# Scaling both banks of a projection into SBUF at once in a hybrid decoder block, with earlier key copies and a longer pause in an inversion

## The chip, the cores and the metric

The kernel runs on one core of one Trainium2 chip. The metric is the device time of one execution in microseconds (us); a kernel's time is the median of several executions.

## What is computed

One decoder layer on 256 tokens with 16 meta tokens put in front (T = 272), width 2048, 16 heads of 128 in each branch, all in float32. The part of the reference that the change touches is the gated DeltaNet branch: the projections of queries, keys and values go through a causal convolution over four tokens and SiLU, and then through a chunked recurrence.

```python
p = rms_norm(h, mix_norm_g) @ w_in
qkv = jax.nn.silu(causal_depthwise_conv(qkv, conv_w))
q, k = l2_normalize(q), l2_normalize(k)
a_mat = jnp.where(strict, jnp.einsum('bhncd,bhnsd->bhncs', k_beta, k) * decay, 0.0)
sol = triangular_solve(a_mat + eye, concat([v * beta, k_beta * exp(g)]))   # unit lower
def step(S, inp):
    v_new = w_val_c - jnp.einsum('bhck,bhkv->bhcv', w_key_c, S)
    o = q_dec_c @ S + qk_c @ v_new
    return S * g_last_c + k_dec_c.T @ v_new, o
```

Beside it stand a forgetting-attention branch (the names with fox), two output projections merged by sigmoid gates, and an MLP with squared ReLU.

## The kernel before

**Matmuls in two parts.** Every weight tile `raw` (128 x 1024) is split into a rounded part `wh` (ScalarE copy, L82) and a rest `wl` (VectorE subtraction, L131); the pool holds three of each, so a `wh` can be written only when TensorE has read the one three tiles earlier for the last time. The activations `u` are split likewise. `gemm_ws` streams 256 weight columns, two heads, over 16 k-tiles into a pair of PSUM banks `acc`, with three matmuls for a k-tile and bank (L168, L169, L170). There are four such banks, two pairs: a gemm writes the banks of the gemm before the last one, and can start in a bank only when that bank has been read.

**Order of the gemms.** Eight for keys, mixed with eight for the fox queries, then eight for queries, eight for V, eight for the fox keys and so on to the MLP.

**Small work between.** What follows a gemm is written as Python generators in a list `tasks`. After each k-tile `pump()` takes one step of each; `pause(n)` lets n steps go by, `until(...)` waits for other tasks. A scheduler then fixes one order of instructions for each engine. Within an engine the order is fixed; between engines semaphores hold it together.

**From bank to convolution.** `conv_silu` multiplies the bank by the row norms `RU` into an SBUF tile `ca` (VectorE, L465), which is the bank's last reader, copies `ca` scaled into `cv` (ScalarE, L82), adds three shifted terms (VectorE, L470) and applies Silu (ScalarE, L472). `ca`, `cv` and the V result `vt` come from a pool of 12 tiles called t272; `kb`, `S`, `y` and other 128-wide tiles from a pool of 10 called t128; a new tile waits until the readers of the one whose buffer it takes are done.

**The V stage.** `value_head` runs once for each head. The odd head of a pair first goes through `pause(10)`, so that its bank is read late. Then come the convolution, a DMA `vb<-vt` and a DMA `kb<-kT` on GpSimd's queue (L90; they copy bits into tiles that TensorE may transpose), transposes by matmul (`flip`, L94) of vb and vs, later of ks and kb, the copies `vnm` and `V` out of PSUM (VectorE, L757, L758), and the recurrence: S, rhs, y, the output in QT and its squares `jk` (ScalarE, L814).

**The inversion.** `invert` solves the 32 x 32 diagonal blocks on VectorE, writes them to DRAM (dY) and back on SyncE's queue (L536, L539), pauses 18 steps, and then builds the larger blocks with small matmuls (L552).

Of the kernel before, what the change touches and what calls it, by code (L numbers as in the profile page):

```python
# [33 lines left out]
def hybrid_block(ctx: ExitStack, tc: tile.TileContext, x, meta_tokens, mix_norm_g, w_in, conv_w, a_log,  # L34
# [23 lines left out]
    def tt(shape, name, dtype=F32):  # L58
        n = 1
        for d in shape[1:]:  # L60
            n *= d
        for size, tag in ((128, "t128"), (272, "t272"), (512, "t512")):
            if n <= size:
                return tmp.tile(shape, dtype, name=name, tag=tag, bufs=TMP_BUFS[tag])
        raise ValueError(n)
# [15 lines left out]
    def acopy(out, in_, scale=1.0):  # L81
        act.activation(out=out, in_=in_, func=AF.Copy, scale=scale)  # L82
# [5 lines left out]
    def bits(src, shape, name, queue=None):  # L88
        dst = tt(shape, name, F32R)
        (queue or nc.gpsimd).dma_start(out=f(dst), in_=src)  # L90
        return dst
# [5 lines left out]
    def stack(dst, src, both):  # L97
        n = list(src.shape)
        one = 1 if both == (0, 2) else 2
        acopy(dst[..., both[0]:both[1] + 1:both[1] - both[0], :], src.unsqueeze(len(n) - 1).broadcast_to(n[:-1] + [2, n[-1]]))  # L100
        dve.tensor_tensor(out=dst[..., one, :], in0=src, in1=f(dst[..., 0, :]), op=ALU.subtract)
# [16 lines left out]
    def until(*names):  # L118
        while not all(n in done for n in names):
            yield  # L120

    def pause(n):
        for _ in range(n):
            yield
# [332 lines left out]
    tasks.append(small_columns())  # L457


    def conv_silu(dst, acc, ct, n, lead):  # L460
        w = [cwT[:, k, ct:ct + 1] for k in range(4)]
        ca, cv = tt([P, T], "ca"), tt([P, T], "cv")
        m = n - lead
        with tc.high_priority():
            dve.tensor_tensor(out=ca[:, 0:n], in0=acc[:, 0:n], in1=RU[:, T - n:T], op=ALU.mult)  # L465
        acopy(cv[:, 0:m], ca[:, lead:n], scale=w[3])
        for d in range(1, 4):
            yield
            off = max(0, d - lead)
            dve.scalar_tensor_tensor(out=cv[:, off:m], in0=ca[:, lead + off - d:n - d], scalar=w[3 - d],  # L470
                                     in1=cv[:, off:m], op0=ALU.mult, op1=ALU.add)
        act.activation(out=dst, in_=cv[:, 0:m], func=AF.Silu)  # L472
# [45 lines left out]
    def invert():  # L518
        I = big_tile([P, 4352], "I")
        N3 = I[:, 0:1024].rearrange("p (r c) -> p r c", c=32)  # L520
        Y3 = I[:, 1024:2048].rearrange("p (r c) -> p r c", c=32)
        YT = I[:, 2048:4096].rearrange("p (a c) -> p a c", c=64)
        dA = dram.tile([4, HT, 32, 32], F32, name="dA")
        for b in range(4):
            nc.sync.dma_start(out=dA[b].rearrange("a r c -> r a c"), in_=XT3[q[b], :, q[b]])
        nc.sync.dma_start(out=N3, in_=dA.rearrange("b a r c -> (b a) r c"))
        identity(Y3, 32)
        yield from pause(18)
        yield from substitute(N3, Y3, I[:, 4096:4352], 32, P)
        dve.tensor_copy(out=N3, in_=Y3.rearrange("p a b -> p b a"))  # L530
        dY = dram.tile([2, 4, HT, 32, 32], F32, name="dY")
        nc.sync.dma_start(out=dY[0].rearrange("b a r c -> (b a) r c"), in_=Y3)
        nc.sync.dma_start(out=dY[1].rearrange("b a r c -> (b a) r c"), in_=N3)
        pool.memset(YT[0:32, :, 32:64], 0.0)
        for b in range(4):
            nc.sync.dma_start(out=XT3[q[b], :, q[b]], in_=dY[0, b].rearrange("a r c -> r a c"))  # L536
            if b < 3:
                cs = slice(32, 64) if b == 1 else slice(0, 32)
                nc.sync.dma_start(out=YT[q[b], :, cs], in_=dY[1, b].rearrange("a r c -> r a c"))  # L539
        yield from pause(18)  # L540

        B1 = [I[:, i * 256:(i + 1) * 256].rearrange("p (a c) -> p a c", c=32) for i in range(2)]
        B2 = [I[:, 1024 + i * 512:1536 + i * 512].rearrange("p (a c) -> p a c", c=64) for i in range(2)]
        G4 = HT // 8
        for step in range(G4 + 3):
            g = [step - i if 0 <= step - i < G4 else None for i in range(4)]
            p1 = ps_tile()[:, 0:256].rearrange("p (a c) -> p a c", c=32)
            p2 = ps_tile()[:, 0:256].rearrange("p (a c) -> p a c", c=32)
            p3 = ps_tile().rearrange("p (a c) -> p a c", c=64)

            def mm(o_, a_, b_):
                pe.matmul(o_, a_, b_, start=True, stop=True)  # L552

            def idx(x, i):
                return 8 * g[x] + i


            for i in range(8):
                if g[2] is not None:
                    mm(p3[hi, i, :], XT3[lo, idx(2, i), hi], YT[lo, idx(2, i), :])  # L560
                if g[3] is not None:
                    mm(p3[lo, i, :], B2[g[3] % 2][hi, i, :], XT3[hi, idx(3, i), hi])
            for i in range(8):
                if g[0] is not None:
                    for b in (0, 2):
                        mm(p1[q[b + 1], i, :], XT3[q[b], idx(0, i), q[b + 1]], YT[q[b], idx(0, i), 0:32])
                if g[1] is not None:
                    b1 = B1[g[1] % 2]
                    mm(p2[q[0], i, :], b1[q[1], i, :], XT3[q[1], idx(1, i), q[1]])
                    mm(p2[q[2], i, :], b1[q[3], i, :], XT3[q[3], idx(1, i), q[3]])  # L570
                    mm(p2[q[1], i, :], XT3[q[1], idx(1, i), q[1]], b1[q[1], i, :])
            js = [slice(8 * x, 8 * x + 8) if x is not None else None for x in g]
            if g[0] is not None:
                for b in (1, 3):
                    acopy(B1[g[0] % 2][q[b]], p1[q[b]])
            if g[1] is not None:
                acopy(XT3[q[0], js[1], q[1]], p2[q[0]], scale=-1.0)
                acopy(YT[q[1], js[1], 0:32], p2[q[1]], scale=-1.0)
                acopy(XT3[q[2], js[1], q[3]], p2[q[2]], scale=-1.0)
            if g[2] is not None:  # L580
                acopy(B2[g[2] % 2][hi], p3[hi])
            if g[3] is not None:
                acopy(XT3[lo, js[3], hi], p3[lo], scale=-1.0)
            yield from pause(3)
        done.add("XT")
# [24 lines left out]
        done.add("XTm")  # L610

    def key_pair(hp, accs):
        for c in range(2):
            h = 2 * hp + c
            yield from conv_silu(kT[:, h, :], accs[c], 16 + h, T, 0)
            if c == 0:
                yield from pause(2)
        yield from pause(4)
# [76 lines left out]
    def query_pair(hp, accs):  # L695
        dst = [QT[:, 2 * hp + c, :] for c in range(2)]
        if "XT" not in done:

            dst = [tt([P, 256], "qt") for c in range(2)]
        for c in range(2):  # L700
            yield from conv_silu(dst[c], accs[c], 2 * hp + c, 260, 4)
            if c == 0:
                yield from pause(2)
        yield from pause(4)
        if "XT" not in done:
            yield from until("XT")
            for c in range(2):
                acopy(QT[:, 2 * hp + c, :], dst[c])
        qb = bits(QT[:, 2 * hp:2 * hp + 2, :], [P, 2, 256], "qb")
        yield from pause(5)  # L710
        ps = ps_tile()
        for c in range(2):
            for t in range(2):
                flip(ps[:, (2 * c + t) * P:(2 * c + t + 1) * P], qb[:, c, t * P:(t + 1) * P])
        for c in range(2):
            for t in range(2):
                jk = tt([P, P], "jk")
                act.activation(out=jk, in_=ps[:, (2 * c + t) * P:(2 * c + t + 1) * P], func=AF.Square,
                               accum_out=ssq[:, t, 2 * hp + c:2 * hp + c + 1])
# [16 lines left out]

    def value_head(h, acc):
        pace = 4
        yield from pause(10 * (h % 2))
        vt = tt([P, T], "vt")  # L740
        yield from conv_silu(vt, acc, 32 + h, T, 0)
        vb = bits(vt[:, NM:T], [P, 256], "vb")
        vs, ks = [tt([P, 3, NM], name, F32R) for name in ("vs", "ks")]
        stack(vs, vt[:, 0:NM], (0, 2))
        stack(ks, kT[:, h, 0:NM], (0, 2))
        kk = [kT[:, h, NM + t * P:NM + (t + 1) * P] for t in range(2)]
        qq = [QT[:, h, t * P:(t + 1) * P] for t in range(2)]
        yield from pause(3)
        yield from until("k", "XT", "XTm")
        kb = bits(kT[:, h, NM:NM + P], [P, P], "kb")  # L750
        ps = ps_tile()
        for t in range(2):
            flip(ps[:, t * P:(t + 1) * P], vb[:, t * P:(t + 1) * P])
# [425 lines left out]
```

## Time and profile before

| | |
|---|---|
| time, median of 3 executions | 1991.64 us (1990.89 to 1992.62) |
| the profiled execution's own time | 1992.09 us |
| its span, first to last instruction | 1990.3 us |
| mean granted TensorE clock | 0.997 |
| TensorE busy | 1966.9 us, 99% |
| VectorE, ScalarE, GpSimd busy | 60%, 51%, 6% |

The time of an execution is its span and under 2 us around it. TensorE's clock has two levels; a granted clock of 1.00 in a stretch is the upper one throughout, 0.50 the lower one.

### The profile page before, as it was taken

To read this page: it belongs to the slowest core of one execution; us is meant where nothing else is said; L and a number is where in the kernel's file an instruction comes from. 1 tells how busy PE (TensorE), PEld (TensorE's weight loads), DVE (VectorE), ACT (ScalarE), POOL (GpSimd) and SP (SyncE) were. 2 spreads that over 40 slices of the span, in tenths; PEclk is the share of its full clock that TensorE was granted. 3 is DMA by queue.
4 is the path that set the end of the run, shared out by engine and by line. 5 is a ranking of instruction groups with operands and counts; after the bars stand their busy time and mean duration, and the time that the engine had idled before them with its cause. 6 is when DMAs were issued, how large, how long until landed. Compare 5 with 4: busy or idle time off the path is not lost.

```text
span 1990.3 us, 30185 instructions
## 1 busy us (share of the span) xinstructions
PE 1966.9 (99%) x11974; PEld 1735.0 (87%) x11974; DVE 1200.4 (60%) x2005; ACT 1008.2 (51%) x1797; POOL 115.1 (6%) x168
## 2 busy tenths in 40 slices
PE   8999999999999999999999999999999999999998
PEld 7898999999999998888888888888888888888886
DVE  5786846677546776644444555566655456665555
ACT  5644466556555555444444445555543345554444
POOL 0022100011131110000000000000000000000000
PEclk9999999999999999999999999999999999999999
DMA  6556766544566545656565666666655566666555
GB/s 201 171 162 204 217 179 205 165 140 141 182 210 198 165 165 200 203 190 201 190 201 190 201 243 212 199 188 188 188 191 193 197 194 186 188 186 212 196 197 176
DMA packets 283139, 378.77 MB, mean 190 GB/s; under 512 B 24163, under 2 KB 190406, under 8 KB 282470
## 3 DMA queue, kind: packets, MB, share of 16 engines
q1 hardware_dynamic: 275584, 353.65, 56.3%
q0 software_dynamic: 7200, 22.92, 3.5%
q8 instruction: 94, 1.54, 0.3%
q14 instruction: 47, 0.39, 0.1%
q10 hardware_dynamic: 214, 0.28, 0.0%
HBM read 351.63 MB, written 3.76 MB: 179 GB/s over the span
## 4 chain that ended last, share of the span: by engine, by line
PE 93%; issue 3%; DMA 2%; DVE 1%; ACT 0%; SPq 0%; POOL 0%; POOLq 0%; DVEq 0%; ACTq 0%
PE acc L165 15%; PE acc L183 15%; PE acc L185 15%; PE acc L184 15%; PE acc L170 14%; PE acc L168 7%; PE acc L169 7%; PE ps L94 1%; DVE wl L131 1%; DMA kb<-kT 1%; PE ps L552 0%; DMA rawS<-in_w_in_dram 0%; PE ps L896 0%; PE ps L628 0%; DMA dY<-I 0%
## 5 line engine op out<-in xcount | busy, mean ns | idle before, releaser
L131 DVE TENSOR_TENSOR wl<-raw,wh 128x1024 fp32r<-128x1024 f32 x644 | 787.7, 1224 | 635.1 <-ACT wh L82 631.8
L82 ACT ACTIVATE wh<-raw 128x1024 fp32r<-128x1024 f32 x644 | 682.1, 1060 | 751.8 <-PE acc L185 463.7
L170 PE MATMUL acc<-u,wl 128*128 128x272 f32 (+2 forms) x1536 | 440.5, 290 | 0.6 <-DVE wl L131 0.6
L168 PE MATMUL acc<-u,wh 128*128 128x272 f32 (+1 forms) x1280 | 373.0, 293 | 1.0 <-DVE ca L465 1.0
L169 PE MATMUL acc<-u,wh 128*128 128x272 f32 (+1 forms) x1280 | 371.8, 291 | 0.0
L165 PE MATMUL acc<-v,wh 128*128 128x512 f32 x1024 | 355.8, 396 | 0.0
L170 PEld LDWEIGHTS acc<-u,wl 128*128 128x128 f32 x1536 | 289.6, 189 | 3.2 <-DVE wl L131 1.2
L170 PE MATMUL acc<-v,wl 128*128 128x256 f32 x1024 | 279.3, 279 | 0.0
L168 PEld LDWEIGHTS acc<-u,wh 128*128 128x128 f32 x1280 | 241.6, 189 | 2.3 <-DVE ca L465 1.5
L169 PEld LDWEIGHTS acc<-u,wh 128*128 128x128 f32 x1280 | 243.0, 190 | 0.7 <-issue 0.2
L165 PEld LDWEIGHTS acc<-v,wh 128*128 128x128 f32 x1024 | 189.5, 188 | 42.8
L184 PE MATMUL acc<-wl,h1h 128*128 128x512 f32 x504 | 196.1, 389 | 0.0
L185 PE MATMUL acc<-wh,h1l 128*128 128x512 f32 x504 | 196.1, 389 | 0.0
L170 PEld LDWEIGHTS acc<-v,wl 128*128 128x128 f32 x1024 | 192.9, 188 | 3.5
L183 PE MATMUL acc<-wh,h1h 128*128 128x512 f32 x504 | 176.3, 389 | 0.0
L185 PE MATMUL acc<-wh,u 128*128 128x512 f32 x384 | 151.6, 395 | 0.0
L184 PE MATMUL acc<-wl,u 128*128 128x512 f32 x384 | 151.1, 394 | 0.0
L183 PE MATMUL acc<-wh,u 128*128 128x512 f32 x384 | 139.2, 396 | 0.0
L183 PEld LDWEIGHTS acc<-wh,h1h 128*128 128x128 f32 x504 | 94.6, 188 | 19.8
L185 PEld LDWEIGHTS acc<-wh,h1l 128*128 128x128 f32 x504 | 94.6, 188 | 19.6
L184 PEld LDWEIGHTS acc<-wl,h1h 128*128 128x128 f32 x504 | 94.6, 188 | 19.4
L165 PE MATMUL acc<-u,wh 128*128 128x512 f32 x256 | 89.5, 395 | 0.0
(378 smaller groups left out, 2387.8 us busy)
## 6 DMA issues: line engine op xcount, KB each, us to landing
raw<-in_w_in_dram SPq DMA_DIRECT2D x142, 1024.0 KB, 5.2
raw<-in_w_down_dram SPq DMA_DIRECT2D x66, 1024.0 KB, 5.2
raw<-in_w_up_dram SPq DMA_DIRECT2D x64, 1024.0 KB, 5.8
raw<-in_w_o_gdn_dram SPq DMA_DIRECT2D x16, 1024.0 KB, 5.2
raw<-in_w_o_fox_dram SPq DMA_DIRECT2D x16, 1024.0 KB, 5.4
raw<-in_w_out_dram SPq DMA_DIRECT2D x16, 1024.0 KB, 5.3
vb<-vt POOLq DMA_DIRECT2D x32, 128.0 KB, 2.2
tb<-tl POOLq DMA_DIRECT2D x16, 208.0 KB, 2.2
```

Of the source, the lines that this page charges most:

```text
L82: act.activation(out=out, in_=in_, func=AF.Copy, scale=scale)
L94: pe.transpose(out=out.bitcast(F32R), in_=in_, identity=identr)
L131: dve.tensor_tensor(out=wl, in0=raw, in1=f(wh), op=ALU.subtract)
L165: pe.matmul(accs[c][:, 0:2 * n].rearrange("p (a n) -> p a n", a=2), wh[:, s], m[kt // 8][:, kt % 8, :, n0:n1], start=(kt == 0), stop=False)
L168: pe.matmul(o, wh[:, s], part(m, kt, 0, n0, n1), start=(kt == 0), stop=False)
L169: pe.matmul(o, wh[:, s], part(m, kt, 1, n0, n1), start=False, stop=False)
L170: pe.matmul(o, wl[:, s], part(m, kt, 0, n0, n1), start=False, stop=(kt == KT - 1))
L183: pe.matmul(accs[t], a, wh, start=(kt == 0), stop=False)
L184: pe.matmul(accs[t], a, wl, start=False, stop=False)
L185: pe.matmul(accs[t], b, wh, start=False, stop=(kt == nkt - 1 - (last if t else 0)))
```

## The change

`normalized` takes the multiplication by `RU` out of `conv_silu`. The three callers run it for both banks of the pair before the first convolution; for a V head it now stands ahead of the odd head's `pause(10)`. The two `ca` tiles of a pair are thus asked for together. In `value_head` the DMA that fills `kb` stands ahead of `pause(3)` and of the wait for the inversion. The second pause in `invert` is 20 steps. The number of instructions of each kind stays the same.

```diff
+    def normalized(acc, n):
+
+        ca = tt([P, T], "ca")
         with tc.high_priority():
             dve.tensor_tensor(out=ca[:, 0:n], in0=acc[:, 0:n], in1=RU[:, T - n:T], op=ALU.mult)
+        return ca
+
+    def conv_silu(dst, ca, ct, n, lead):
+        w = [cwT[:, k, ct:ct + 1] for k in range(4)]
+        cv = tt([P, T], "cv")
+        m = n - lead
         acopy(cv[:, 0:m], ca[:, lead:n], scale=w[3])
...
-        yield from pause(18)
+        yield from pause(20)
...
     def key_pair(hp, accs):
+        cas = [normalized(acc, T) for acc in accs]
         for c in range(2):
             h = 2 * hp + c
-            yield from conv_silu(kT[:, h, :], accs[c], 16 + h, T, 0)
+            yield from conv_silu(kT[:, h, :], cas[c], 16 + h, T, 0)
...
+        cas = [normalized(acc, 260) for acc in accs]
         for c in range(2):
-            yield from conv_silu(dst[c], accs[c], 2 * hp + c, 260, 4)
+            yield from conv_silu(dst[c], cas[c], 2 * hp + c, 260, 4)
...
     def value_head(h, acc):
         pace = 4
+        ca = normalized(acc, T)
         yield from pause(10 * (h % 2))
         vt = tt([P, T], "vt")
-        yield from conv_silu(vt, acc, 32 + h, T, 0)
+        yield from conv_silu(vt, ca, 32 + h, T, 0)
...
+        yield from until("k")
+        kb = bits(kT[:, h, NM:NM + P], [P, P], "kb")
...
         yield from until("k", "XT", "XTm")
-        kb = bits(kT[:, h, NM:NM + P], [P, P], "kb")
```

The line numbers of the changed kernel differ: the multiplication into `ca` is L464 there, the V copies L766 and L767, the recurrence L780 to L823.

**TensorE between two V gemms.** In the kernel before, one gemm (acc_5616 and acc_5617, the last weight tile wh_5827) passes into the next (acc_5894) like this:

```order
L168 MATMUL acc_5616<-u1_141,wh_5827 128x272
L169 MATMUL acc_5616<-u1_141,wh_5827 128x272
L170 MATMUL acc_5616<-u1_141,wl_5828 128x272
L168 MATMUL acc_5617<-u1_141,wh_5827 128x272
L785 MATMUL ps_5673<-ptm0_4209 128x128
L169 MATMUL acc_5617<-u1_141,wh_5827 128x272
L170 MATMUL acc_5617<-u1_141,wl_5828 128x272
L806 MATMUL ps_5704<-y_5632,kq_5228 128x128
L799 MATMUL ps_5709<-rhs_5637,XT_171 128x128
L168 MATMUL acc_5894<-u0_140,wh_5898 128x272
```

Behind the last L170 of acc_5617 two small matmuls stand. In the changed kernel the same gemm's banks are called acc_5618 and acc_5619, and the next gemm's acc_5896. Its last L170 is followed by the eight rows L800, L801, L794, L814, L815, L780, L786 x2 and L808 of the recurrence, and then by:

```order
L800 MATMUL ps_5636<-S_5567,kT_170 128x128
L801 MATMUL ps_5636<-S_5567,QT_3030 128x128
L94 MATMUL ps_5642<-identr_94,vb_5578 128x128 x2
L94 MATMUL ps_5642<-identr_94,vs_5580 48x128
L800 MATMUL ps_5669<-S_5597,kT_170 128x128
L801 MATMUL ps_5669<-S_5597,QT_3030 128x128
L794 MATMUL ps_5675<-ptm0_4209 128x128
L815 MATMUL ps_5708<-y_5634,kq_5230 128x128
L808 MATMUL ps_5713<-rhs_5639,XT_171 128x128
L94 MATMUL ps_5717<-identr_94,ks_5581 48x128
L94 MATMUL ps_5717<-identr_94,kb_5586 128x128
L168 MATMUL acc_5896<-u0_140,wh_5900 128x272
```

From the last matmul of one gemm to the first of the next there are 20 small rows now; the transposes of vb_5578 and vs_5580, which before stood among the gemm's last k-tiles, are between the gemms.

**ScalarE at the same place.** Before, around the Silu of the odd head (vt_5537), whose DMA fills vb_5578:

```order
L814 ACTIVATE jk_5524,oss_3032<-QT_3030 128x128
L82 ACTIVATE y_5528<-ps_5526 128x128
L82 ACTIVATE kd_5535<-ps_5530,kds_164 128x128
L82 ACTIVATE wh_5827<-raw_5757 128x1024
L472 ACTIVATE vt_5537<-cv_5539 128x272
L82 ACTIVATE S_5567<-ps_5565 128x128
L82 ACTIVATE vs_5580<-vt_5537 128x2x16
L82 ACTIVATE ks_5581<-kT_170 128x2x16
L82 ACTIVATE wh_5898<-raw_5896 128x1024
```

And in the changed kernel (vt_5539; wh_6039 takes the buffer of wh_5827, which the gemm's last matmuls read):

```order
L823 ACTIVATE jk_5526,oss_3032<-QT_3030 128x128
L82 ACTIVATE y_5530<-ps_5528 128x128
L82 ACTIVATE kd_5537<-ps_5532,kds_164 128x128
L82 ACTIVATE wh_6039<-raw_6037 128x1024
L82 ACTIVATE S_5567<-ps_5565 128x128
L477 ACTIVATE vt_5539<-cv_5540 128x272
L82 ACTIVATE QT_3030<-ps_5559,eG_165 128x128
L82 ACTIVATE ptm0_4209<-ps_5602,kds_164 48x128
L82 ACTIVATE xs0_4211<-XTs_173 48x48
L82 ACTIVATE vs_5580<-vt_5539 128x2x16
L82 ACTIVATE ks_5581<-kT_170 128x2x16
```

The Silu stood behind wh_5827 and now stands behind wh_6039, a weight tile of the next gemm.

**VectorE ahead of a gemm's start.** Before, the multiplication that frees the second bank for acc_5617 (ca_5538, from acc_5061) stood behind the V copies of the even head:

```order
L101 TENSOR_TENSOR ks_5411<-kT_170,ks_5411 128x16
L794 SCALAR_TENSOR_TENSOR rhs_5461<-ps_5458,neG_166,V_5192 128x128
L757 CAST vnm0_4207<-ps_5466 48x128
L758 TENSOR_TENSOR V_5470<-ps_5466,nrk_177 128x256
L809 SCALAR_TENSOR_TENSOR S_5494<-S_5289,eGl_163,ps_5491 128x128
L812 TENSOR_TENSOR QT_3030<-ps_5491,QT_3030 128x128
L773 SCALAR_TENSOR_TENSOR ptm1_4210<-ps_5499,kds_164,ptm1_4210 16x128
L780 SCALAR_TENSOR_TENSOR kq_5506<-ps_5503,cst_176,DT_168 128x128
L465 TENSOR_TENSOR ca_5538<-acc_5061,RU_139 128x272
```

Now the one that frees the first bank for acc_5896 (ca_5649, from acc_5340) stands behind the V copies of the odd head:

```order
L782 SCALAR_TENSOR_TENSOR ptm0_4209<-ps_5602,kds_164,ptm0_4209 16x128
L101 TENSOR_TENSOR vs_5580<-vt_5539,vs_5580 128x16
L101 TENSOR_TENSOR ks_5581<-kT_170,ks_5581 128x16
L803 SCALAR_TENSOR_TENSOR rhs_5639<-ps_5636,neG_166,V_5368 128x128
L766 CAST vnm1_4208<-ps_5642 48x128
L767 TENSOR_TENSOR V_5646<-ps_5642,nrk_177 128x256
L464 TENSOR_TENSOR ca_5649<-acc_5340,RU_139 128x272
L803 SCALAR_TENSOR_TENSOR rhs_5672<-ps_5669,neG_166,V_5194 128x128
L821 TENSOR_TENSOR QT_3030<-ps_5708,QT_3030 128x128
L464 TENSOR_TENSOR ca_5654<-acc_5341,RU_139 128x272
```

What moved: before, only the second bank of a gemm was freed behind such V copies; now both banks of a gemm are.

## Rows read from the trace of the kernel before

**Rows 1.** The page, part 1: busy us (share of the span) and count, TensorE.
```profile
PE 1966.9 (99%) x11974; PEld 1735.0 (87%) x11974; DVE 1200.4 (60%) x2005; ACT 1008.2 (51%) x1797; POOL 115.1 (6%) x168
```

**Rows 2.** Waits of TensorE, whole span: us in total, times, longest.
```profile
PE ps L94 <- DMA kb<-kT: 2.9, 6, 1.1
PE ps L552 <- DMA I<-dY: 1.3, 1, 1.3
PE acc L168 <- DVE ca L465: 1.0, 2, 0.9
```

**Rows 3.** Windows: length, each engine's busy us (count), granted clock, DMA share, GB/s.
```profile
20.00:25.00 5.00, 3.79 (x19) 3.13 (x20) 3.81 (x6) 2.62 (x4) 0.00 (x0) 0.66 0.66 190
401.00:420.00 19.00, 17.67 (x145) 17.18 (x144) 13.51 (x34) 10.43 (x35) 2.14 (x4) 1.00 0.43 137
```

**Rows 4.** Timeline of TensorE, 405 to 410 us: start, length, instruction, [idle before <-releaser].
```profile
405.88 0.34 PE L94 MATMUL ps<-identr,vb 128*128 128x128 f32 x2 [0.20 <-DMA vb<-vt]
406.06 0.23 PE L94 MATMUL ps<-identr,vs 128*48 128x128 f32 x1
...
409.20 0.29 PE L94 MATMUL ps<-identr,kb 128*128 128x128 f32 x1 [1.13 <-DMA kb<-kT]
```

**Rows 5.** Timeline of TensorE, one V gemm later.
```profile
425.64 0.29 PE L170 MATMUL acc<-u,wl 128*128 128x272 f32 x1
425.77 0.28 PE L94 MATMUL ps<-identr,vb 128*128 128x128 f32 x2
...
428.24 0.28 PE L94 MATMUL ps<-identr,kb 128*128 128x128 f32 x1 [0.35 <-DMA kb<-kT]
428.38 0.39 PE L168 MATMUL acc<-u,wh 128*128 128x272 f32 x1
```

**Rows 6.** Timeline of ScalarE in the V stage.
```profile
400.22 1.06 ACT L82 ACTIVATE wh<-raw 128x1024 fp32r<-128x1024 f32 x1
401.18 0.26 ACT L82 ACTIVATE ptm<-ps 48x128 fp32r<-48x128 f32 x1
...
403.04 0.43 ACT L472 ACTIVATE vt<-cv 128x272 f32<-128x272 f32 x1 [1.60 <-DVE cv L470]
...
419.95 0.26 ACT L82 ACTIVATE S<-ps 128x128 f32<-128x128 f32 x1
420.10 0.36 ACT L82 ACTIVATE QT<-ps,eG 128x128 f32<-128x128 f32 x1
```

**Rows 7.** Timeline of VectorE in the V stage.
```profile
406.32 0.28 DVE L757 CAST vnm<-ps 48x128 fp32r<-48x128 f32 x1 [2.26 <-PE ps L94]
406.53 0.41 DVE L758 TENSOR_TENSOR V<-ps,nrk 128x256 f32<-128x256 f32 x1
406.86 0.33 DVE L809 SCALAR_TENSOR_TENSOR S<-S,eGl,ps 128x128 f32<-128x128 f32 x1
...
427.89 0.43 DVE L465 TENSOR_TENSOR ca<-acc,RU 128x272 f32<-128x272 f32 x1
```

**Rows 8.** Timeline of GpSimd, which issues these DMAs.
```profile
403.76 0.54 POOL L90 DMA_DIRECT2D vb<-vt  x1 [10.31 <-ACT vs L82]
406.58 0.53 POOL L90 DMA_DIRECT2D kb<-kT  x1 [2.28 <-PE ps L94]
...
426.41 0.53 POOL L90 DMA_DIRECT2D kb<-kT  x1 [3.34 <-PE ps L94]
```

**Rows 9.** Timeline of all engines at 62 us.
```profile
62.40 0.43 DVE L443 COPY th<-ps 32x272 f32<-32x272 f32 x1 [2.85 <-PE ps L441]
62.75 0.76 DVE L465 TENSOR_TENSOR ca<-acc,RU 128x272 f32<-128x272 f32 x2
...
63.23 0.39 PE L168 MATMUL acc<-u,wh 128*128 128x272 f32 x1 [0.87 <-DVE ca L465]
```

**Rows 10.** Timeline of TensorE at the first inversion matmul.
```profile
260.37 0.31 PE L552 MATMUL ps<-I,XT 32*32 32x32 f32 x4 [1.29 <-DMA I<-dY]
```

**Rows 11.** Timeline of TensorE after its wait near the start.
```profile
20.68 0.33 PE L338 MATMUL acc<-u,wh 128*48 128x272 f32 x1 [1.91 <-ACT wh L82]
```

More of the change, by code (lines that the diff above doesn't have):

```diff
@@ L457, in hybrid_block @@
     tasks.append(small_columns())
[L460 to L463, printed above, removed]
+    def normalized(acc, n):
+        ca = tt([P, T], "ca")
         with tc.high_priority():
             dve.tensor_tensor(out=ca[:, 0:n], in0=acc[:, 0:n], in1=RU[:, T - n:T], op=ALU.mult)
+        return ca
[3 more added lines that the diff above has]
+        m = n - lead
         acopy(cv[:, 0:m], ca[:, lead:n], scale=w[3])
```

## Prediction, made before the changed kernel ran

> **What bounds the kernel now.** I read the busy shares first: TensorE works 1966.9 us, 99% of the span [rows 1], so a change can win only what TensorE waits, and loses whatever it makes it wait. The list of TensorE's waits comes next. The three that the edits aim at are the key copy kb (2.9 us in six waits, the longest 1.1), the multiplication into `ca` (1.0 us, nearly all in one wait) and the inversion's read-back from DRAM (1.3 us in one) [rows 2]. Together that is 5.2 us, 0.26% of the time: the most that the change can win. The six kb waits lie in the V stage, where nothing else idles for long; TensorE's clock is at its upper level there [rows 3]. Then I went to the timelines of that stage, for TensorE, ScalarE, VectorE and GpSimd together, since there the edits change the order most.
>
> One V gemm follows another every 19.04 us (the kb transpose of one pair at 409.20, of the next at 428.24 [rows 4, 5]).
>
> **Key banks scaled together.** At 62.40 VectorE waits 2.85 us for TensorE's transpose of G; the multiplication that frees a bank stands behind it at 62.75, and TensorE waits 0.87 us for it [rows 9]. In the new order both banks of that key pair are asked for together, and the gemm's first matmul no longer stands right behind this copy. I take the whole 0.9 as won: bounds 0, if another `ca` is just as late, and 1.0, all waits of that kind [rows 2]. For the query pairs no such wait is listed, so TensorE's own gemm covers them: nothing won; the price without that cover is the `ca` step, 0.5 us a pair at most (427.89 to 428.38 [rows 5, 7]).
>
> **Key copies.** kb's DMA is issued at 406.58, after GpSimd has waited 2.28 us for the transpose of vs, which gives back the buffer [rows 8]. Its transpose comes at 409.20 with 1.13 us of waiting; a gemm later at 428.24 with 0.35 [rows 4, 5]. Issued ahead of the pauses, it lands before it is wanted: bound 2.9 us won [rows 2]. But `ca` started at 427.89 and the gemm's second bank at 428.38, 0.49 later [rows 5, 7], which is a step from one engine to the next: without kb the 0.35 would have been VectorE's. So 1.1 is firmly to be had, 2.9 is the upper end.
>
> **Pause of 20.** The order of SyncE's queue is the same to the last row, and the first inversion matmul stands behind the same seven matmuls of the query gemm, with the same wait for the DMA (1.29 us at 260.37 [rows 10]). I cost this edit at 0; its ends are 0 and 1.3 won.
>
> **The V stage: a new wait.** This is the largest term. Before, the odd head's bank is freed late, so a gemm's second bank runs alone at the end of the overlap and the gemms pass into each other with two small matmuls between. Now 20 small rows stand there, and no matmul of a gemm lies among them to fill a wait. Two things hold them up. The first matmul of acc_5896 needs ca_5649, which stands on VectorE behind the copies vnm1_4208 and V_5646, and these need the transposes of vb_5578 and vs_5580. And vb_5578 hangs on the Silu vt_5539, which stands on ScalarE behind wh_6039; that one takes the buffer of wh_5827, which the ending gemm reads to its last matmuls. Counted from the start of the L169 before the last L170:
>
> - ScalarE starts wh_6039 0.26 later, as VectorE starts 0.26 after the matmul that it waits for (406.06, 406.32 [rows 4, 7]);
> - wh holds ScalarE 0.96 (400.22 to 401.18) and S 0.15 (419.95 to 420.10) [rows 6];
> - from the Silu's start to the issue of vb's DMA 0.72 (403.04 to 403.76), from there to its transpose 2.12 (403.76 to 405.88) [rows 4, 6, 8].
>
> That is 4.21 us to the transpose of vb. Behind it VectorE's way is 0.18 to the transpose of vs, 0.26 to vnm, 0.21 to V, 0.33 to ca and 0.49 to the matmul, 1.47 [rows 4, 5, 7]. TensorE's own way is 14 matmul records (a float32 row counts as two, a transpose of one tile as one). A row of small matmuls goes at (428.38 - 425.77 - 0.35) / 18 = 0.126 us each, 18 being the records between those rows [rows 5]; 14 make 1.76. The longer of the two counts, so the next gemm starts 4.21 + 1.76 = 5.97 us after that L169.
>
> Without the wait it would be two steps of a gemm matmul (425.64 to 425.77, 0.13 each [rows 5]) and 34 records (20 ahead of the transposes), 0.26 + 4.27 = 4.53. The new wait is thus 1.44 us for each transition. Behind it queue the recurrence's next steps on all engines, and nothing gives the time back, since the next gemm itself starts later. Its lower bound is 0, if the order's two dependences are met sooner than these rows say. The upper one is 1.9: a DMA of GpSimd's queue took 0.5 longer to its transpose in kb's case (406.58 to 409.20, 2.62 [rows 4, 8]).
>
> There are six transitions. In the four steady ones and the last one the wait comes (1.44) and kb's goes (0.35): +1.1 each, 5.5 together. In the first one the Silu isn't behind a weight tile, and fewer rows of the recurrence stand ahead of vb's transpose to cover its DMA; I take a wait as long as the kb wait that goes there (1.13), so 0, with 1.1 to either side. So the V stage loses 5.5 us, kb's gain already counted.
>
> VectorE's row at 62.40 shows an engine that keeps its order: the ready multiplication stood behind a copy that waited 2.85 us [rows 9]. The Trainium skill (PSUM — Partial Sum Buffer, section Engine vs sequencer instructions) says it of all three: the queues of ScalarE, VectorE and GpSimd are strictly first in, first out, and matmuls start and end in program order. The trace agrees on VectorE. Were it otherwise on ScalarE, so that the Silu went ahead of wh_6039, the chain would be 0.26 + 0.96 = 1.22 shorter, the wait 0.2, and the sum about 1990; by the rule it is the sum below.
>
> **Sum.** Against the profiled execution's 1992.09: -0.9 for the key banks, +5.5 in the V stage, 0 for the rest: 1996.7. That execution lies 0.45 above the median, so for the median 1996.2 us, 0.23% above 1991.64. A measurement of this kernel can tell about 0.2%, 4 us, from no change, so the forecast stands right at that bound.
>
> **Rivals.**
> - *The copies arrive in time* (other side). If the Silu and vb's DMA come 1.44 us sooner than the chain says, no transition waits. For it: kb's waits and the 0.87 at 63.23 are real and their causes gone. Against it: 2.12 from issue to transpose was seen with TensorE already waiting 0.20 [rows 4], so it hardly shrinks. Time: 1991.64 - 0.9 - 1.1 to - 2.9 = 1987.8 to 1989.6, and 1986.5 with the inversion's wait gone as well. It decides for faster when the wait at a transition is below 0.2 us.
> - *Cancelled*: the wait is about half as long (0.7), 5 x 0.35 - 0.9 = +0.9; 1990 to 1994.
> - *The clock falls.* Near the start TensorE waited 1.91 us at 20.68 [rows 11], and the window from 20 to 25 us ran at a granted clock of 0.66, the lower of its two levels for about two thirds of it; at full work that costs 0.34 x 5 = 1.7 us [rows 3]. Each new cluster of small matmuls with a wait in it could bring that on: five times 1.7 on top, 2004.7; once or twice, 1998 to 1999.6. Against it: the cluster with 1.13 us of waiting left the clock at 1.00 [rows 3, 4], and the new wait is between the two. The Trainium skill (TensorE: Matmul & The Clock Gate, section HAM oscillation — how this bites in real kernels) describes matmul bursts with waits between, where the clock falls anew at every one. By that rule the last case would hold at all five; the trace agrees with it at 20 us and not at 409.
> - *The pause does nothing*: this is part of my sum; were it otherwise, 1.3 less.
>
> **How the numbers follow.** The new wait without a fall of the clock 0.58 (1994 to 1998.5, the centre 1996.2, about two thirds of it above 1995.6); the clock falls at some transitions 0.17 (1998 to 2004.7); cancelled 0.10; copies in time 0.15 (1986.5 to 1990). The range leaves out the lower two thirds of the last (0.1) and the highest third of the clock's case (0.06), with a little for what I don't see: 1989 to 2002. Slower by over 0.2% (above 1995.6): 0.38 + 0.17 = 0.55. Faster by over 0.2% (below 1987.7): 0.08, half of the copies in time. Within: 0.37.
>
> **What would show it.** In the new profile the kb waits of L94 are gone, and among TensorE's waits stands one on DMA vb<-vt (L94) or on DVE ca (L464) at the gemm transitions, some 1.4 us, five times, every 20 us instead of 19. The wait for ca at 63 us is gone; the inversion's 1.3 stays. The V stage's windows keep a granted clock of 1.00, or else the clock's case holds. I am wrong if transitions come every 19 us or sooner, if the Silu of an odd head starts before the ending gemm's last matmul, or if a wait that I don't name is over 2 us.

## The result and the profile after

The changed kernel takes 2001.80 us (median of 4 executions, 2000.34 to 2006.20) against 1991.27 us of the kernel before on the same chips: a ratio of 1.0053, with an interval from 1.0036 to 1.0070. The profiled execution has a span of 1999.0 us, 8.7 more than before, and TensorE's work has hardly changed (1966.9 before [rows 1]):

```profile
PE 1968.9 (98%) x11974; PEld 1735.4 (87%) x11974; DVE 1200.7 (60%) x2005; ACT 1013.2 (51%) x1801; POOL 114.1 (6%) x168
```

Two things stand in this line. Most of the loss is waiting, not work. And ScalarE has four instructions more (1801; the page before counts 1797), though no step was added: that the number of instructions of each kind stays the same does not hold for ScalarE. Its groups by line show them, before (L472 is Silu there) and now: 9 loads of a function table, 5 for Silu (L477) and 4 for the decays' exponentials (L374), where the kernel before had 3 and 2.

```profile
L472 ACT ACT_TABLE_LOAD x3 | 3.8, 1283 | 0.0
L374 ACT ACT_TABLE_LOAD x2 | 2.6, 1283 | 0.0
...
L477 ACT ACT_TABLE_LOAD x5 | 6.4, 1283 | 0.1
L374 ACT ACT_TABLE_LOAD x4 | 5.1, 1283 | 0.1
```

TensorE's waits (us in total, times, longest), to be held against [rows 2]:

```profile
PE acc L168 <- ACT wh L82: 3.5, 1, 3.5
PE ps L800 <- DVE QT L821: 2.2, 5, 0.5
...
PE ps L786 <- ACT S L82: 1.4, 4, 0.4
PE ps L94 <- DVE ptm L782: 1.4, 1, 1.4
PE ps L94 <- DVE vs L101: 1.1, 3, 0.4
PE ps L557 <- DMA I<-dY: 1.0, 1, 1.0
```

The six waits for kb are gone, and so is the 0.87 for `ca` at 63 us. The inversion's wait is still there (1.0, 1.29 before [rows 10]). New are one wait for a weight tile, 3.5 us, and fifteen waits of up to 1.4 us in the V stage, 7.4 us together.

**Where the time went.** The start of each gemm can be read from TensorE's timeline (its first L168). From the start of the second key gemm to that of the first query gemm it is 198.2 us before (39.0 to 237.2) and 199.3 now: the early stage loses 1.1 where 0.9 was to be won. From the fourth V gemm to the last fox-key gemm but one it is 190.6 before (384.3 to 574.9) and 199.0 now (384.7 to 583.7): the V stage loses 8.4. Behind that nothing changes. (The query stage between is 0.3 longer, and the second key gemm starts 1.0 sooner, at 38.0, so that these parts make up the 8.7.) The V stage's windows (length, busy us and count of each engine, granted clock, DMA share, GB/s) show that one share of it is the clock, one fall across two of them, 3% and 6% of 20 us, some 1.8 us; the windows from 441 to 521 stand at 1.00:

```profile
401.00:421.00 20.00, 18.64 (x148) 18.13 (x148) 13.27 (x31) 11.08 (x35) 2.13 (x4) 0.97 0.51 164
421.00:441.00 20.00, 19.49 (x146) 18.52 (x145) 13.49 (x33) 11.69 (x37) 2.13 (x4) 0.94 0.39 123
```

**One transition between two V gemms.** The timelines of TensorE, ScalarE, VectorE and GpSimd, one behind the other:

```profile
478.33 0.29 PE L170 MATMUL acc<-u,wl 128*128 128x272 f32 x1
...
480.05 0.71 PE L786 MATMUL ps<-QT,kT 128*128 128x128 f32 x4 [0.36 <-ACT S L82]
...
481.60 0.49 PE L800 MATMUL ps<-S,kT 128*128 128x128 f32 x2 [0.49 <-DVE QT L821]
...
482.68 0.33 PE L94 MATMUL ps<-identr,vb 128*128 128x128 f32 x2 [0.36 <-DVE vs L101]
...
484.29 0.36 PE L168 MATMUL acc<-u,wh 128*128 128x272 f32 x1
...
478.77 1.05 ACT L82 ACTIVATE wh<-raw 128x1024 fp32r<-128x1024 f32 x1
479.72 0.27 ACT L82 ACTIVATE S<-ps 128x128 f32<-128x128 f32 x1
479.88 0.44 ACT L477 ACTIVATE vt<-cv 128x272 f32<-128x272 f32 x1
...
479.86 1.23 DVE L131 TENSOR_TENSOR wl<-raw,wh 128x1024 fp32r<-128x1024 f32 x1 [0.41 <-ACT wh L82]
481.00 0.34 DVE L818 SCALAR_TENSOR_TENSOR S<-S,eGl,ps 128x128 f32<-128x128 f32 x1
...
482.47 0.18 DVE L101 TENSOR_TENSOR vs<-vt,vs 128x16 fp32r<-128x16 f32 x1
...
483.65 0.42 DVE L464 TENSOR_TENSOR ca<-acc,RU 128x272 f32<-128x272 f32 x1
...
480.61 0.54 POOL L90 DMA_DIRECT2D vb<-vt  x1 [12.83 <-ACT QT L82]
```

The predicted chain is there step by step: wh, S, the Silu behind them at 479.88, the issue of vb 0.73 later, its transpose 2.07 after that. The next gemm starts at 484.29, 6.09 us after the L169 of 478.20 (one step of 0.13 ahead of the L170 shown); 5.97 was forecast. But the transpose of vb is put down to VectorE's vs, not to the DMA. VectorE has a chain of its own that ends within 0.1 us of the DMA's landing (1.9 us after its issue): the other half of the same weight tile's split, wl, which holds VectorE from 479.86 on, then S from 481.00, QT, kq, ptm, and vs at 482.47. The prediction had only one of these two chains. Nor is there one wait at the transposes: of TensorE's 1.21 us of waiting here only 0.36 stands there, and 0.85 at rows of the recurrence ahead of them, for S and QT, which the prediction let run without a wait.

**The wait at 95 us.** ScalarE's timeline from 89 us, then TensorE's:

```profile
89.17 0.61 ACT L374 ACTIVATE DT<-DT 128x512 f32<-128x512 f32 x1
89.80 1.28 ACT L477 ACT_TABLE_LOAD   x1
91.09 0.43 ACT L477 ACTIVATE kT<-cv 128x272 f32<-128x272 f32 x1
91.43 0.92 ACT L82 ACTIVATE cv<-ca,cwT 128x272 f32<-128x272 f32 x2
92.36 1.28 ACT L374 ACT_TABLE_LOAD   x1
93.66 0.63 ACT L374 ACTIVATE DT<-DT 128x512 f32<-128x512 f32 x1
94.19 1.04 ACT L82 ACTIVATE wh<-raw 128x1024 fp32r<-128x1024 f32 x1
...
95.28 0.39 PE L168 MATMUL acc<-u,wh 128*128 128x272 f32 x1 [3.55 <-ACT wh L82]
```

ScalarE isn't idle for a moment here. Silus of keys and exponentials of the decays alternate, each change loads a table for 1.28 us, and the weight tile that TensorE needs comes last.

### The profile page after: what moved, and what is told of

It reads as the page before. It is cut to its first block, busy times and chain, and to the rows that moved or that the text cites. A ratio compares the mean times of both kernels' runs of the same rounds, so it can differ in the third digit from the quotient of the medians.

```text
span 1999.0 us, 30215 instructions
## 1 busy us (share of the span) xinstructions
PE 1968.9 (98%) x11974; PEld 1735.4 (87%) x11974; DVE 1200.7 (60%) x2005; ACT 1013.2 (51%) x1801; POOL 114.1 (6%) x168
## 4 chain that ended last, share of the span: by engine, by line
PE 93%; DVE 2%; DMA 2%; ACT 1%; issue 1%; SPq 0%; POOL 0%; POOLq 0%; DVEq 0%; ACTq 0%
PE acc L185 15%; PE acc L183 15%; PE acc L184 15%; PE acc L170 14%; PE acc L165 14%; PE acc L168 7%; PE acc L169 7%; PE ps L94 1%; DVE wl L131 1%; ACT wh L82 1%; PE ps L557 0%; DMA rawS<-in_w_in_dram 0%; PE ps L634 0%; PE ps L905 0%; DMA dY<-I 0%
## 5 line engine op out<-in xcount | busy, mean ns | idle before, releaser
L170 PE MATMUL acc<-u,wl 128*128 128x272 f32 (+2 forms) x1536 | 439.7, 289 | 0.0
L168 PE MATMUL acc<-u,wh 128*128 128x272 f32 (+1 forms) x1280 | 370.4, 291 | 3.7 <-ACT wh L82 3.5
L169 PE MATMUL acc<-u,wh 128*128 128x272 f32 (+1 forms) x1280 | 370.4, 290 | 0.0
L170 PEld LDWEIGHTS acc<-u,wl 128*128 128x128 f32 x1536 | 289.7, 189 | 2.3 <-issue 0.4
L170 PE MATMUL acc<-v,wl 128*128 128x256 f32 x1024 | 279.3, 279 | 0.0
L168 PEld LDWEIGHTS acc<-u,wh 128*128 128x128 f32 x1280 | 240.8, 189 | 4.8 <-ACT wh L82 4.0
L169 PEld LDWEIGHTS acc<-u,wh 128*128 128x128 f32 x1280 | 242.2, 189 | 0.8 <-issue 0.2
L170 PEld LDWEIGHTS acc<-v,wl 128*128 128x128 f32 x1024 | 192.9, 188 | 3.5
```

Source lines behind the costliest of these rows:

```text
L168: pe.matmul(o, wh[:, s], part(m, kt, 0, n0, n1), start=(kt == 0), stop=False)
L169: pe.matmul(o, wh[:, s], part(m, kt, 1, n0, n1), start=False, stop=False)
L170: pe.matmul(o, wl[:, s], part(m, kt, 0, n0, n1), start=False, stop=(kt == KT - 1))
```

## Experiments

The times are medians; each ratio is to the kernel before on the same chip, with its interval. The table gives, from the trace of each kernel, the time from one gemm's first L168 to the next one's, from the fifth V gemm on (six gemms in a row):

```
kernel                                     us from gemm to gemm
before                                     19.38 19.10 19.12 19.09 19.12 19.17
changed                                    21.91 20.80 20.50 20.45 20.62 20.01
V heads alone                              20.13 21.96 22.42 21.25 24.03 22.45
copies alone                               18.84 19.34 19.37 19.33 19.36 18.98
V heads and copies                         21.10 20.52 20.48 20.47 20.50 20.00
  the same, pause of 6                     20.02 20.71 20.75 20.76 20.78 18.88
  the same, pause of 6, without wl         18.91 19.37 19.38 20.51 20.75 18.92
  the same, pause of 10, without wl        19.13 19.26 20.32 20.90 20.43 21.18
  the same, own pool for ca                15.38 16.62 16.80 15.70 20.14 39.26
keys (later decay), copies, pause of 8     19.51 18.81 18.83 18.81 18.83 18.01
```

### The parts alone

Each kernel starts from the changed one and takes the other parts back. `normalized` is then called where the convolution starts, which gives the order of the kernel before:

```diff
-        cas = [normalized(acc, T) for acc in accs]
...
-            yield from conv_silu(kT[:, h, :], cas[c], 16 + h, T, 0)
+            yield from conv_silu(kT[:, h, :], normalized(accs[c], T), 16 + h, T, 0)
```

**Key pairs alone.**

> Only the key pairs scale both banks at once; the rest is as in the kernel before. Theory (queue on ScalarE): the loss in the early stage belongs to this edit alone. The order of ScalarE has 16 table loads instead of 12, so a wait for wh of 3 to 4 us stands near 95 us, the waits for ca at 63 and for wl at 70 and 82 are gone, V gemms follow every 19.1 us as before; time 1991 to 1994. Rival (the prediction's term): the wait at 95 was an accident of one execution, 0.9 won, 1990.6.

1992.61 us, ratio 1.0007 (0.9999 to 1.0016). The wait for the weight tile is there again, 3.55 us at 97.85, so it was no accident. From the second key gemm to the first query gemm this kernel takes 199.3 us (39.07 to 238.34), 1.1 more than before, and its gemms in the V stage follow every 19.1 us as before.

**V heads alone.**

> Only the V heads scale their bank at once. Theory (both banks of a gemm behind the odd head's chain): 18 small rows in a row at each V transition, gemms every 20.3 to 20.7 us instead of 19.1, the V stage 6 to 9 us longer, nothing else changed; time 1997.5 to 2000.5. Rival (the key copies ahead of vb on GpSimd's queue make the wait, the banks don't): under 1994.

2006.31 us, ratio 1.0075 (1.0058 to 1.0092): dearer than expected, and dearer than the whole change. Its profile is that of the slowest of its executions, 2012.03 us. Waits of TensorE, and the window of the V stage:

```profile
PE ps L94 <- DVE rhs L800: 5.1, 3, 1.7
PE ps L94 <- DMA vb<-vt: 4.8, 3, 2.0
...
400.00:533.00 133.00, 121.78 (x928) 118.32 (x927) 86.98 (x216) 72.22 (x228) 12.85 (x24) 0.94 0.39 121
```

TensorE waits 10 us for vb and for rhs, and the clock falls in this stage (0.94 over 133 us; at full speed the stage would hold some 8 us less). The odd heads' vb takes 4.4 to 4.8 us from issue to landing at the transitions from 435 us on, where the changed kernel has 1.9 to 2.3; why is not shown. The rival that the copies make the wait is out: without them it is worse.

**Copies alone.**

> Only the key copies are early. Theory: the six kb waits (2.9 us) go; part of that is taken by ca, which is 0.5 us from being the releaser, so 1.1 to 2.9 won: 1988.5 to 1990.4. Rival (copies ahead of vb delay its transposes): waits for vb in the place of those for kb, 1991.5 to 1994.

1992.24 us, ratio 1.0003 (0.9994 to 1.0012): nothing won, where 1.1 to 2.9 was expected. The six waits for kb are gone, and others have taken their place:

```profile
PE acc L168 <- DVE ca L464: 3.4, 8, 0.9
...
PE ps L783 <- ACT QT L82: 1.7, 6, 0.3
...
448.38 0.39 PE L168 MATMUL acc<-u,wh 128*128 128x272 f32 x1 [0.40 <-DVE ca L464]
```

That is the cover that the prediction named, `ca` half a microsecond behind kb. It took all of the gain, more than was allowed for: gemms follow every 19.35 us instead of 19.11. The rival's time was met, but not its cause: no wait for vb is among TensorE's.

**V heads and copies together.**

> V heads scale at once and copies are early; key and query pairs and the pause as before. Theory: the V stage of the changed kernel, 8 to 9 us longer than before, and nothing else, so 1999 to 2000.5; against the V heads alone no gain from the copies, since a wait for vb stands where kb's was. Rival (the parts simply add): the V heads' loss less what the copies win alone.

1999.82 us, ratio 1.0045 (1.0030 to 1.0060). In its profile the clock never falls in the V stage, and the stage (fourth V gemm to last fox-key gemm but one) still takes 197.8 us (383.8 to 581.6), 7.2 more than before. So without any fall of the clock the new order costs about 7 of the 8.4 us that the changed kernel's V stage loses. The parts don't add: the copies win nothing alone, and 6.5 us in the medians beside the V heads. Much of that is the clock: the V stages of the two profiles are 9.6 us apart (207.4 and 197.8), and the clock makes some 8 of it; at the same mean clock of 0.997 one execution of the V heads alone took 2001.86 and one with the copies 1999.70.

### The early stage: table loads on ScalarE

**Key pairs alone, decays later.** Edit:

```diff
-        yield from pause(30)
+        yield from pause(36)
         decay(DTm, G[:NM, 0, 0:H], NM)
```

> The key pairs alone, with the pause ahead of the decays' exponentials 36 instead of 30 steps, which leaves 14 table loads in ScalarE's order instead of 16. Theory (the queue of table loads, exponentials and Silus ahead of a weight tile is what TensorE waits for near 95 us): two loads of 1.28 us fewer take 2.5 us from the wait for wh of 3.5, which becomes 1 or less; time 1.5 to 2.5 under the key pairs alone in the trace, 1989.5 to 1991.5. Rival (the tile is late for another reason, its load from DRAM or the banks): the wait stays at 3 or more.

1988.23 us, ratio 0.9984 (0.9975 to 0.9993): faster than the kernel before, and by more than was expected. Two table loads are gone from the key stage, and of the wait 0.19 is left:

```profile
L477 ACT ACT_TABLE_LOAD x4 | 5.1, 1283 | 0.1
L374 ACT ACT_TABLE_LOAD x3 | 3.8, 1283 | 0.1
...
91.95 0.39 PE L168 MATMUL acc<-u,wh 128*128 128x272 f32 x1 [0.19 <-ACT wh L82]
...
40.00:100.00 60.00, 59.65 (x441) 55.83 (x440) 49.85 (x131) 44.05 (x62) 4.63 (x6) 1.00 0.64 196
```

TensorE is busy 59.65 of the 60 us from 40 to 100. Before it was 57.87 there, and 56.29 in the changed kernel, each with one fall of the clock in that window (0.97). So part of the gain in this profile is the clock: from the second key gemm to the first query gemm it takes 194.9 us (38.1 to 233.0), 3.3 less than before, and 0.03 of 60 us is 1.8. That the tile is late for its load or its banks is out, since neither changed. Whether the later decays win as much without the key pairs was not run.

**The whole change, decays later.**

> The changed kernel with the pause ahead of the decays 36 instead of 30 steps, 14 table loads instead of 16. Theory: the wait for wh near 95 us goes, as with the key pairs alone, and nothing else changes: 3.5 to 5 less than the changed kernel, 1996.5 to 1998.5. Rival: in the whole change the gain is eaten in the V stage: 2000 or more.

1997.27 us, ratio 1.0032 (1.0021 to 1.0044): 4.5 us under the changed kernel's median, as expected, though the two intervals overlap. In the trace the stretch from the second key gemm to the first query gemm is 196.2 us (38.9 to 235.1) instead of 199.3. The V stage keeps its loss (20.0 to 21.2 a gemm; 198.0 us from 382.3 to 580.3), here again without a fall of the clock.

### The V stage: what the transition waits for

**An earlier Silu.** On top of V heads and copies, the odd head's pause is 6:

```diff
-        yield from pause(10 * (h % 2))
+        yield from pause(6 * (h % 2))
```

> V heads scale at once and early copies, as before, but the odd head pauses 6 steps instead of 10. In the order its Silu then stands two weight tiles earlier on ScalarE, so that the copy vb has landed long before its transpose, and 10 small rows stand between two gemms instead of 19. Theory (the wait is the chain from the ending gemm's last weight tile over Silu and vb): the wait of 1.4 goes, V gemms follow every 18.6 to 19.2 us, time 1990 to 1992.5. Rival (any block of small rows between gemms waits, whatever the Silu): 19.7 or more a gemm, 1995 or more.

2000.76 us, ratio 1.0044 (1.0032 to 1.0056). The theory of the prediction falls here as the only cause. The Silu is early, TensorE waits for no vb, 10 small rows stand between the gemms, and a gemm still takes 20.75. VectorE's timeline at a transition, then TensorE's:

```profile
481.30 1.21 DVE L131 TENSOR_TENSOR wl<-raw,wh 128x1024 fp32r<-128x1024 f32 x1
...
483.18 0.43 DVE L464 TENSOR_TENSOR ca<-acc,RU 128x272 f32<-128x272 f32 x1
...
482.94 0.24 PE L94 MATMUL ps<-identr,ks 128*48 128x128 f32 x1 [0.87 <-DVE ptm L780]
...
483.66 0.40 PE L168 MATMUL acc<-u,wh 128*128 128x272 f32 x1 [0.40 <-DVE ca L464]
```

The rest wl of the tile that had to wait for the ending gemm stands ahead of ptm and of the `ca` that frees the bank.

**Without that subtraction.** From the second to the last V gemm wl isn't computed, and TensorE's third matmul reads an older one:

```diff
-            dve.tensor_tensor(out=wl, in0=raw, in1=f(wh), op=ALU.subtract)
+            if rest["on"]:
+                dve.tensor_tensor(out=wl, in0=raw, in1=f(wh), op=ALU.subtract)
...
+        rest["on"] = hp == 0
         accs = gemm_ws(win, C_V + hp * 256, u, 0, T)
+        rest["on"] = True
```

> As the V heads with copies and a pause of 6, but from the second V gemm to the last the rest wl is not subtracted on VectorE (the third matmul reads an old wl instead), so this part of the values is left out; the order keeps 10 small rows between gemms. New theory: with the Silu early, the wait at the transition is VectorE's queue, in which the split of the weight tile that waits for the ending gemm (wl, 1.2 us) stands ahead of ptm and of the ca that frees the bank. Without it the V gemms follow every 19.4 to 19.8 us instead of 20.76. Rival (the block of dependent small rows takes that long by itself): 20.4 or more.

The execution holds its own comparison: no wl is split in the first three intervals of its row in the table; in the later ones it is, since the fox-key gemms split as ever, the first of their tiles already at the end of the last V gemm. 18.91, 19.37 and 19.38 us without, 20.51 and 20.75 with (20.75 in the kernel above). So 1.1 to 1.4 us a gemm go with this subtraction, and the block of ten small rows by itself costs little. That it is the one at the transition which counts is read from the rows, since the others of a gemm were left out as well. (The time, 1994.46 us, ratio 1.0018, leaves that work out.) A transition without wl, where TensorE's first matmul still waits a little for ca, and one with it:

```profile
437.45 0.43 DVE L469 TENSOR_TENSOR ca<-acc,RU 128x272 f32<-128x272 f32 x1
...
437.93 0.39 PE L173 MATMUL acc<-u,wh 128*128 128x272 f32 x1 [0.22 <-DVE ca L469]
...
475.45 1.20 DVE L136 TENSOR_TENSOR wl<-raw,wh 128x1024 fp32r<-128x1024 f32 x1
...
477.09 0.25 PE L94 MATMUL ps<-identr,ks 128*48 128x128 f32 x1 [0.74 <-DVE ptm L785]
...
477.82 0.39 PE L173 MATMUL acc<-u,wh 128*128 128x272 f32 x1 [0.40 <-DVE ca L469]
```

**The same at the pause of 10.**

> As the V heads with early copies at the pause of 10, with the same subtraction left out; 19 small rows stand between gemms as before. Theory of the prediction (ScalarE's wh, then S, Silu, vb's DMA, its transpose): that chain is untouched by VectorE, so gemms follow every 20.2 to 20.6 us as with it (20.48), and the wait at the transpose of vb is put down to the DMA. Rival (only VectorE's queue counts): 19.6 or less.

1997.47 us, ratio 1.0043 (1.0029 to 1.0057), with that work left out. The first two gemms without wl take 19.13 and 19.26, the third 20.32, those with it again 20.43 to 21.18. That was to be a test of ScalarE's chain by itself, and it is not one: with fewer instructions the order came out with the Silu ahead of the weight tile (450.24 and 450.90 in ScalarE's timeline), so both chains were shortened at once. What it shows is that with both out of the way a gemm takes what it took before, although 19 small rows stand between, except where the DMA itself was slow, as in the third:

```profile
454.88 0.33 PE L94 MATMUL ps<-identr,vb 128*128 128x128 f32 x2 [1.31 <-DMA vb<-vt]
...
450.96 0.54 POOL L90 DMA_DIRECT2D vb<-vt  x1 [10.91 <-PE acc L174]
```

3.92 us from issue to transpose instead of 2.07. How much of the changed kernel's wait would be left with VectorE's chain alone removed stays open.

**An own pool for ca.** On top of V heads and copies:

```diff
-TMP_BUFS = {"t128": 10, "t272": 12, "t512": 4}
+TMP_BUFS = {"t128": 10, "t272": 9, "t512": 4}
...
+        ca = tmp.tile([P, T], F32, name="ca", tag="tca", bufs=3) if own else tt([P, T], "ca")
```

> V heads scale at once and early copies, with the V heads' ca tiles in a pool of their own of 3 buffers and t272 of 9. In the order no small rows stand between the first five V gemms, and 53 between the last ones. Theory (the banks are freed late only since the ca tiles wait for buffers that the odd head's chain holds): gemms with nothing between follow every 18.9 us or sooner and the loss moves to the end of the stage, where 53 rows at 0.2 to 0.3 us with their waits, 11 to 16 us instead of 6.7 at the closest step, cost 5 to 9; time 1990 to 1998. Rival (buffers don't matter): gemms every 20 us or more from the second on.

2000.29 us, ratio 1.0047 (1.0035 to 1.0059). As the theory of the buffers says, no small rows hold up the first gemms, 15.4 to 16.8 us each, and the small work piles up at the end, where the last interval is 39.26 us. The loss is larger than expected. At the pile the transposes wait for vb's DMA (7.1 us in three waits), and the window has a clock of 0.91, some 3.5 of its 39 us:

```profile
508.59 0.47 PE L94 MATMUL ps<-identr,vb 128*128 128x128 f32 x2 [2.70 <-DMA vb<-vt]
...
485.00:524.00 39.00, 30.66 (x222) 28.99 (x223) 24.84 (x75) 21.22 (x76) 4.96 (x10) 0.91 0.26 82
```

Early banks let gemm matmuls run ahead of the small work that they were to cover.

### A version that beats both

Key pairs at once with the later decays, early copies, and the V heads scaled one at a time as before, with `pause(8 * (h % 2))`.

> Key pairs at once with the later decay, early copies, V heads scaled one at a time as before but with a pause of 8 instead of 10. In the order 8 and 5 small rows stand between runs of gemm matmuls instead of 10 and 2. Theory: the ca that stood in for kb as the releaser with early copies comes two k-tiles sooner, so the 0.4 a gemm that TensorE waits for it goes; V gemms every 18.7 to 19.1 us, time 1985.5 to 1988.5. Rival: smaller blocks at two places wait as much: 19.3 or more, 1988.5 to 1990.5.

1987.55 us, ratio 0.9983 (0.9973 to 0.9993). In the V stage gemms follow every 18.82 us instead of 19.11, as expected, and TensorE is busy 18.88 of 19 us (18.60 to 18.66 in the windows before):

```profile
420.00:439.00 19.00, 18.88 (x158) 18.58 (x158) 14.53 (x37) 11.76 (x39) 2.31 (x5) 1.00 0.43 132
```

Against the key pairs with later decays alone (0.9984) the two intervals can't be told apart; what is shown of the second gain is the trace, 0.3 us a gemm.

## Why the prediction was right, and where its sizes were off

Slower was forecast, by 4.6 us, and 10.5 was measured; the time lies 0.2 us inside the upper edge of the range. The direction and the largest term were understood. That the time is still in the range is partly luck: the range went so far up for the case of a falling clock, and the clock made under 2 us of the loss in the profile shown, while an early stage that lost where a gain was put and a transition put at 0 made the rest of the excess. Two of the signs that the prediction set for itself came out otherwise: a wait that it doesn't name is over 2 us (3.5, for the weight tile), and in place of five waits of 1.4 us for vb or ca there are several smaller ones for S, QT and vs.

- **The V stage's new wait**, the largest term, came where it was put and by the instructions that were named: the next gemm 6.09 us after the last L169 (5.97 forecast), the kb waits gone. Its size was 5.5 and is 7.2 without a fall of the clock. In the four steady transitions 1.4 to 1.5 came instead of 1.1 (1.7 in the one into which the clock's fall reaches) and 0.8 in the last, partly since ScalarE was still busy with kd when the tile's buffer came free (wh started 0.57 after that L169, not 0.26). That 6.09 comes so near to 5.97 holds two errors that partly cancel: the transpose of vb 4.48 after that L169 (4.21 forecast), and 1.61 from there to the gemm (1.76). The first transition was set to 0; it is 1.7 in the kernel with V heads and copies (21.10 against 19.38), the largest single miss of the term.
- **The cause of that wait** was half named. The weight tile that takes the ending gemm's buffer holds up two queues: ScalarE's by wh (ahead of the Silu) and VectorE's by wl (ahead of ptm, vs and ca). The prediction followed the first. With the Silu moved out of it the wait stayed, and without the subtraction 1.1 to 1.4 us a gemm went.
- **"Key banks scaled together: I take the whole 0.9 as won"** failed. The waits at 63 us and after it went, but the Silus of the keys came into the stretch in which the decays' exponentials run. Four more table loads of 1.28 us stood in ScalarE's order, and a weight tile came 3.55 us late. The early stage lost 1.1. The prediction read the new order at that place for the bank and for TensorE, not for ScalarE, where these loads stand. They were no part of the sum, and no rival had them.
- **Key copies**: the waits went as forecast. That the gain might be VectorE's next was said (1.1 to 2.9); alone it is none.
- **The pause of 20** does nothing that shows: the wait is 1.0 where it was 1.29, and it is 1.0 in the V heads alone too, where the pause is 18.
- **The clock** was a rival at 0.17 for one or more transitions. It fell once in the V stage of the profile shown (some 1.8 us), never there in those of V heads and copies and of the whole change with later decays, whose V stages lose 7.2 and 7.4 all the same, and over and over in that of V heads alone. So it was a part of the loss and not its cause. (In executions that were not profiled it may have been more: one of the changed kernel's took 2006.20 at a mean clock of 0.995, where the other three are at 0.997, and one of V heads and copies 2007.65 at 0.993.) Nor does a wait by itself bring it on: the 1.9 us at 20 us that the prediction took as its example are there in the changed kernel too, and the window from 20 to 25 us now stands at 1.00 (the line is at the end). At the first V transition TensorE waits 1.4 us in the changed kernel and 1.4 in that with V heads and copies; the clock fell in the first and held in the second. The Trainium skill (TensorE: Matmul & The Clock Gate, section HAM oscillation — how this bites in real kernels) tells of a fall at every one of the waits between its bursts, and its waits are longer than the ones here; in this trace the clock fell at one of six.
- **That the queues keep their order** carries both losses: a Silu behind wh, ptm and ca behind wl, wh behind table loads. The Trainium skill (PSUM — Partial Sum Buffer, section Engine vs sequencer instructions) states it for the three engines, and these traces agree on ScalarE and VectorE.

## What to carry to other kernels

When a gemm's banks are freed earlier, ask what then has to cover the small work: here it was the late second bank that let gemm matmuls run beside it, and freeing it early put the small work between the gemms. A tile whose buffer the ending gemm gives back last is a bad neighbour in every queue in which its preparation stands ahead of small steps; follow it on all engines, not on the first one found. And when steps move by a few microseconds, count the table loads in ScalarE's new order: two functions that come to alternate cost more than the wait that the move took away.

## What the runs showed of the hardware that was not expected

A change of function on ScalarE took 1.28 us each time, more than the 0.43 us of the Silu for which it was made, and 16 of them instead of 12 held up a weight tile by 3.55 us. A DMA of 128 KB on GpSimd's queue took 2.07 us from issue to its transpose at one transition and 3.92 at another in a second kernel, with the same bytes; from issue to landing it was 1.9 at the first of these, and up to 4.8 with the V heads alone. And the clock fell in one kernel and held in another behind like waits of TensorE: at 20 us behind 1.9 us (0.66 in the window before the change, 1.00 after it), and at the first V transition behind 1.4 us (it fell in the changed kernel, and stood at 1.00 with V heads and copies). The window at 20 us in the changed kernel, to be held against [rows 3]:

```profile
20.00:25.00 5.00, 3.53 (x26) 2.90 (x26) 3.95 (x7) 2.84 (x4) 0.00 (x0) 1.00 0.66 190
```
